# The Hyena short convolution kept in the order of the tokens, with TensorE's transposes taking every eighth column of it

## The chip, the cores and the metric

The kernel runs on one core of a Trainium2 chip. The metric is the device time of one execution in microseconds; the profile is one execution taken by the hardware profiler. Its engines are TensorE (PE, with its weight loads as PEld), VectorE (DVE), ScalarE (ACT), GpSimd (POOL) and SyncE (SP), which issues the DMAs.

## The reference, cut to what matters

One layer of an encoder: a SwiGLU half, a mixer of a Hyena branch and an RWKV-7 branch, another SwiGLU half, on 1024 tokens of 1024 features in float32. The change lies in the first step of the Hyena branch, a convolution of width three along the tokens, for each of 1536 channels, and in the layout in which its result is handed to the long convolution.

```python
def _centred_conv3(u, w, b):
    up = jnp.pad(u, ((0, 0), (1, 1), (0, 0)))
    return w[0] * up[:, :-2] + w[1] * up[:, 1:-1] + w[2] * up[:, 2:] + b
...
    uc = _centred_conv3(u, conv_w, conv_b).astype(jnp.float32)
    x1, x2, v = jnp.split(uc, 3, axis=-1)
```

## The kernel before, in words

The mixer's input projection is computed column tile by column tile. A tile is 128 channels; `column` multiplies it out for two halves of 512 tokens with split float32r operands (`mm3`, lines 43 to 45), 24 matmuls into each PSUM bank `pw`, of which there are three. The first twelve tiles are the Hyena ones, in the order 8 to 11 (v), 0 to 3 (x1) and 4 to 7 (x2). Behind each of them stands `hyena_short_conv`.

In that function the channels lie on the partitions and the tokens along the free dimension. ScalarE copies each half out of PSUM into `u` (tile `sh_u`, line 505, with a zero column at either end), and writes the middle tap with its bias into `uc` (tile `sh_o`, line 506). VectorE adds the two outer taps, one instruction for each over all 1024 tokens (line 509). Then TensorE transposes `uc` in eight blocks of 128 x 128 (line 515; the block is the stationary operand, which a weight load brings in, and the identity is what moves), four to a PSUM bank (`hy_tp`), ScalarE copies each bank out (line 516) and one DMA writes the tile to DRAM (line 517).

The long convolution behind it works on tokens n = 8 m + r, with m on the partitions and r = 0 to 7 along the free dimension (`RT` is 8). So block r of the transposes must hold the tokens r, r + 8, r + 16 and so on. In the kernel before, `uc` has the shape [128, 8, 128] with r outermost. Lines 506 and 509 write it (and line 509 reads it) through the view `ucv`, whose next element in the order of the tokens lies 128 floats (512 bytes) further; each transposed block is contiguous.

Between the column tiles the program computes the Hyena filters in steps (`hyena_filters`): matmuls `ps_h` (line 376) and `ps_k` (line 404) on TensorE, `kt`, `eo`, `cxt` and `kout` on VectorE, `sq` on ScalarE, `acc` on GpSimd, and DMAs of `kout` to DRAM (`d_kf`). GpSimd also makes the low halves of the weights (`w_lo`, line 37) for the first nine of these tiles. A scheduler sets the order of the instructions on each engine when the program is built; on the chip each engine goes through its own list in order. The RWKV column tiles follow (`rwkv_columns`, `rwkv_tile`): they have the same copy out of PSUM and the same two VectorE taps, in the order of the tokens on both sides (lines 1249 and 1258, tiles also named `sh_u` and `sh_o`).

Of the kernel before, what the change touches and what calls it, by code (L numbers as in the profile page):

```python
# [13 lines left out]
F32 = mybir.dt.float32  # L14
F32R = mybir.dt.float32r
AF = mybir.ActivationFunctionType
ALU = mybir.AluOpType
# [3 lines left out]
P = 128  # L21
L = 1024
# [225 lines left out]
RT = 8  # L248
# [247 lines left out]
def hyena_short_conv(nc, pool, xpool, psum, ident, ps, cw, dst):  # L496


    u = pool.tile([P, L + 2], F32, name="sh_u", tag="sh_u")
    nc.vector.memset(u[:, 0:1], 0.0)  # L500
    nc.vector.memset(u[:, L + 1 : L + 2], 0.0)
    uc = pool.tile([P, RT, P], F32, name="sh_o", tag="sh_o")
    ucv = uc.rearrange("p r m -> p m r")
    for t in range(2):
        nc.scalar.copy(u[:, 1 + 512 * t : 513 + 512 * t], ps[t])
        nc.scalar.activation(ucv[:, ts(t, 64), :], ps[t].rearrange("p (m r) -> p m r", r=RT),
                             AF.Identity, bias=cw[:, 3:4], scale=cw[:, 1:2])
    for j in (0, 2):
        nc.vector.scalar_tensor_tensor(ucv, u[:, j : j + L].rearrange("p (m r) -> p m r", r=RT),
                                       cw[:, j : j + 1], ucv, ALU.mult, ALU.add)  # L510
    o = xpool.tile([P, RT, P], F32, name="sh_x", tag="sh_x")
    for h in range(2):
        pt = psum.tile([P, 4, P], F32, name="hy_tp", tag="hy_tp")
        for q in range(4):
            nc.tensor.transpose(pt[:, q], uc[:, 4 * h + q, :], ident)
        nc.scalar.copy(o[:, 4 * h : 4 * h + 4, :], pt)
    nc.sync.dma_start(dst, o)

# [661 lines left out]
def mixer_in(tc, I, ident, wp, hl, scl, h2, h2ctx, dr):  # L1180
# [3 lines left out]
    with ExitStack() as ctx:  # L1184
# [110 lines left out]
        with ExitStack() as c2:  # L1295
            ptp = c2.enter_context(tc.tile_pool(name="hytp", bufs=2, space=PSUM))
            sx = c2.enter_context(tc.tile_pool(name="shx", bufs=2))
            cw = hyena_vectors(nc, one, I)
            hidden = hyena_hidden(tc, I, h2)
            done = 0  # L1300

            for i, t in enumerate((8, 9, 10, 11, 0, 1, 2, 3, 4, 5, 6, 7)):
                if i < 2:
                    next(hidden)
                elif i == 2:
                    for _ in hidden:
                        pass
                    bg = hyena_filters(tc, c2, I, h2, dr["kf"], scl)
                while i > 1 and (done < i * 3 or (t < 8 and t // 2 >= scl.filters)):
                    if next(bg, bg) is bg:  # L1310
                        break
                    done += 1
                ps = column(t * P)
                if t < 8:
                    nc.vector.tensor_scalar(cw[:, t], cw[:, t], scl.tile[:, t : t + 1], None, ALU.mult)
                hyena_short_conv(nc, two, sx, ptp, ident, ps, cw[:, t], dr["X"][t // 4][:, :, ts(t % 4, P)])
            for _ in bg:
                pass
# [426 lines left out]
```

## Time and profile before

| | |
|---|---|
| median of 3 runs | 2900.08 us (2899.32 to 2900.85) |
| the profiled execution | 2905.31 us, its span 2903.5 us |
| PE busy | 2718.3 us, 94% of the span |
| DVE busy | 1232.0 us, 42% |
| ACT busy | 905.1 us, 31% |
| POOL busy | 555.4 us, 19% |
| mean granted TensorE clock | 0.966 |

The span runs from the first instruction to the last; the 1.8 us between it and the execution's time lie around it. A busy share is an average over the whole program: the twelve Hyena tiles take about a tenth of it. A wait is put down to whatever released it last.

### The profile page before, as it was taken

The page shows a single profiled execution, that of the slowest core. Times are in us where ns is not written, and L with a number is a line of the kernel's source. Part 1 is how long each engine was busy: PE and PEld are TensorE (multiplying, and loading weights), DVE is VectorE, ACT ScalarE, POOL GpSimd, SP SyncE. Part 2 cuts the span into 40 slices and gives each one's busy share as a digit, 9 for nine tenths or more (in the row PEclk, how much of TensorE's full clock was granted, in tenths as well). Part 3 has the DMA queues.
Part 4 walks back from the last instruction along what each step waited for, and adds up shares of the span by engine and source line. Part 5 has one row for each costly group of instructions (what it writes and reads, how often), then busy time and mean ns, then how long its engine had stood idle before and what let it go on. Part 6 is the DMA issues. An engine that isn't in the chain of part 4 may idle for free. (4 is left out here: it accounts for less than half of the span.)

```text
span 2903.5 us, 46061 instructions
## 1 busy us (share of the span) xinstructions
PE 2718.3 (94%) x19440; PEld 2198.2 (76%) x19440; DVE 1232.0 (42%) x2141; ACT 905.1 (31%) x1517; POOL 555.4 (19%) x351
## 2 busy tenths in 40 slices
PE   7999999999689899987899999797999999999998
PEld 6888888888566677775787787675778888888887
DVE  4111110111547669898765566756560111101014
ACT  4111111111445443333554555522332111111112
POOL 2323233232414210000000000000033232223322
PEclk9999999999899999998999999898999999999999
DMA  4111111111342245554445334457631111111102
GB/s 123 51 44 51 44 55 47 41 54 41 112 134 69 91 129 179 149 168 127 135 125 160 102 113 148 145 161 234 189 87 54 49 51 44 55 40 53 48 27 91
DMA packets 408990, 277.49 MB, mean 96 GB/s; under 512 B 51107, under 2 KB 369135, under 8 KB 408144
## 3 DMA queue, kind: packets, MB, share of 16 engines
q1 hardware_dynamic: 408784, 274.55, 31.7%
q8 instruction: 153, 2.51, 0.4%
q14 instruction: 53, 0.43, 0.0%
HBM read 203.58 MB, written 70.91 MB: 95 GB/s over the span
## 5 line engine op out<-in xcount | busy, mean ns | idle before, releaser
L43 PE MATMUL pgu<-hThi,w_hi 128*128 128x512 f32 x1408 | 554.1, 394 | 0.8 <-issue 0.8
L45 PE MATMUL pgu<-hThi,w_lo 128*128 128x512 f32 x1408 | 551.4, 392 | 0.0
L44 PE MATMUL pgu<-hTlo,w_hi 128*128 128x512 f32 x1408 | 548.4, 390 | 0.5 <-DVE hTlo L37 0.3
L210 DVE TENSOR_TENSOR silu<-silu,pgu 128x512 f32<-128x512 f32 x88 | 60.5, 688 | 892.2 <-PE pgu L45 882.7
L33 ACT CAST w_hi<-w_st 128x1024 fp32r<-128x1024 f32 (+1 forms) x180 | 175.5, 976 | 496.2 <-PE pgu L44 320.4
L37 POOL TENSOR_TENSOR w_lo<-w_st,w_hi 128x1024 fp32r<-128x1024 f32 x100 | 240.4, 2404 | 413.2 <-ACT w_hi L33 407.5
L45 PEld LDWEIGHTS pgu<-hThi,w_lo 128*128 128x128 f32 x1408 | 264.6, 188 | 60.5
L44 PEld LDWEIGHTS pgu<-hTlo,w_hi 128*128 128x128 f32 x1408 | 264.6, 188 | 59.1 <-DVE hTlo L37 0.7
L43 PEld LDWEIGHTS pgu<-hThi,w_hi 128*128 128x128 f32 x1408 | 264.7, 188 | 55.8 <-issue 1.2
L43 PE MATMUL pdn<-g_hi,wd_hi 128*128 128x512 f32 x704 | 274.9, 391 | 4.6 <-DVE xT L227 4.6
L44 PE MATMUL pdn<-g_lo,wd_hi 128*128 128x512 f32 x704 | 274.4, 390 | 2.0 <-POOL g_lo L37 2.0
L45 PE MATMUL pdn<-g_hi,wd_lo 128*128 128x512 f32 x704 | 274.8, 390 | 1.5 <-POOL wd_lo L37 1.5
L227 DVE SCALAR_TENSOR_TENSOR xT<-pdn,xT 128x512 f32<-128x512 f32 x192 | 132.4, 691 | 315.3 <-PE pdn L45 315.3
L43 PE MATMUL pw<-hThi,w_hi 128*128 128x512 f32 (+1 forms) x448 | 186.4, 416 | 18.5 <-DVE nm_h L123 10.0
L45 PE MATMUL pw<-hThi,w_lo 128*128 128x512 f32 (+1 forms) x448 | 186.8, 418 | 12.1 <-DVE w_lo L1228 12.1
L37 POOL TENSOR_TENSOR wd_lo<-wdst,wd_hi 128x512 fp32r<-128x512 f32 (+1 forms) x112 | 132.9, 1187 | 332.8 <-ACT wd_hi L33 332.8
L37 POOL TENSOR_TENSOR g_lo<-silu,g_hi 128x512 fp32r<-128x512 f32 x88 | 113.9, 1294 | 397.2 <-ACT g_hi L33 397.2
L44 PE MATMUL pw<-hTlo,w_hi 128*128 128x512 f32 (+1 forms) x448 | 184.6, 412 | 0.0
L33 ACT CAST wd_hi<-wdst 128x512 fp32r<-128x512 f32 (+1 forms) x112 | 64.4, 576 | 379.1 <-PE pdn L44 360.7
L37 POOL TENSOR_TENSOR hTlo<-nm_h,hThi 128x512 fp32r<-128x512 f32 x16 | 23.1, 1444 | 802.9 <-ACT hThi L33 802.9
L43 PEld LDWEIGHTS pdn<-g_hi,wd_hi 128*128 128x128 f32 x704 | 132.2, 188 | 33.2 <-ACT wd_hi L33 4.0
L44 PEld LDWEIGHTS pdn<-g_lo,wd_hi 128*128 128x128 f32 x704 | 132.2, 188 | 30.8 <-POOL g_lo L37 2.9
(312 smaller groups left out, 4245.5 us busy)
## 6 DMA issues: line engine op xcount, KB each, us to landing
w_st<-in_ffn_w_gu SPq DMA_DIRECT2D x88, 512.0 KB, 3.9
w_st<-in_w_in SPq DMA_DIRECT2D x59, 512.0 KB, 4.2
wdst<-in_ffn_w_down SPq DMA_DIRECT2D x64, 256.0 KB, 2.8
wdst<-in_ffn_w_down SPq DMA_DIRECT2D x48, 192.0 KB, 2.5
d_kf<-kout SPq DMA_DIRECT2D x32, 256.0 KB, 2.2
hy_k<-d_kf SPq DMA_DIRECT2D x32, 256.0 KB, 3.2
w_st<-in_w_out SPq DMA_DIRECT2D x16, 512.0 KB, 4.4
d_X<-sh_x SPq DMA_DIRECT2D x12, 512.0 KB, 3.5
```

The costliest lines, as they stand in the source:

```text
L33: nc.scalar.copy(hi, src)
L37: eng.tensor_tensor(lo, src, hi.bitcast(F32), ALU.subtract)
L43: te.matmul(out, lhs[0], rhs[0], start=first, stop=False)
L44: te.matmul(out, lhs[0], rhs[1], start=False, stop=False)
L45: te.matmul(out, lhs[1], rhs[0], start=False, stop=last)
L210: nc.vector.tensor_tensor(sl, sl, pu, ALU.mult)
L227: nc.vector.scalar_tensor_tensor(xa, ps, 0.5, xa, ALU.mult, ALU.add)
```

## The change

`uc` becomes a plain [128, 1024] tile in the order of the tokens. Lines 506 and 509 now write and read it contiguously. The reordering moves to the transposes: block r takes the columns r, r + 8, r + 16 and so on, 128 floats that lie 8 floats (32 bytes) apart, as the stationary operand.

```diff
-    uc = pool.tile([P, RT, P], F32, name="sh_o", tag="sh_o")
-    ucv = uc.rearrange("p r m -> p m r")
+    uc = pool.tile([P, L], F32, name="sh_o", tag="sh_o")
     for t in range(2):
         nc.scalar.copy(u[:, 1 + 512 * t : 513 + 512 * t], ps[t])
-        nc.scalar.activation(ucv[:, ts(t, 64), :], ps[t].rearrange("p (m r) -> p m r", r=RT),
-                             AF.Identity, bias=cw[:, 3:4], scale=cw[:, 1:2])
+        nc.scalar.activation(uc[:, ts(t, 512)], ps[t], AF.Identity, bias=cw[:, 3:4], scale=cw[:, 1:2])
     for j in (0, 2):
-        nc.vector.scalar_tensor_tensor(ucv, u[:, j : j + L].rearrange("p (m r) -> p m r", r=RT),
-                                       cw[:, j : j + 1], ucv, ALU.mult, ALU.add)
+        nc.vector.scalar_tensor_tensor(uc, u[:, j : j + L], cw[:, j : j + 1], uc, ALU.mult, ALU.add)
     o = xpool.tile([P, RT, P], F32, name="sh_x", tag="sh_x")
     for h in range(2):
         pt = psum.tile([P, 4, P], F32, name="hy_tp", tag="hy_tp")
         for q in range(4):
-            nc.tensor.transpose(pt[:, q], uc[:, 4 * h + q, :], ident)
+            nc.tensor.transpose(pt[:, q], uc[:, 4 * h + q :: RT], ident)
         nc.scalar.copy(o[:, 4 * h : 4 * h + 4, :], pt)
```

The numbers of the lines below fall by three; the same instructions stand in the same places of every engine's list. This is VectorE's list around the third tile, before (-) and after (+); `hhx` is a tile of the filters' small network.

```order
 L284 SCALAR_TENSOR_TENSOR hhx<-hhx 64x512
 L285 TENSOR_SCALAR hhx<-hhx 64x512
-L509 SCALAR_TENSOR_TENSOR sh_o<-sh_u,hy_cw,sh_o 128x128x8
+L507 SCALAR_TENSOR_TENSOR sh_o<-sh_u,hy_cw,sh_o 128x1024
 L281 TENSOR_SCALAR hhx<-hhx 64x512
-L509 SCALAR_TENSOR_TENSOR sh_o<-sh_u,hy_cw,sh_o 128x128x8
+L507 SCALAR_TENSOR_TENSOR sh_o<-sh_u,hy_cw,sh_o 128x1024
 L282 TENSOR_SCALAR hhx<-hhx 64x512
```

Nothing moved: the two taps stand where they stood, and only the shape in which they go over the tile is another.

## Rows read from the trace of the kernel before

**Rows 1.** The page: its first line, and the busy time of each engine with its share of the span and its instructions.

```profile
span 2903.5 us, 46061 instructions
...
PE 2718.3 (94%) x19440; PEld 2198.2 (76%) x19440; DVE 1232.0 (42%) x2141; ACT 905.1 (31%) x1517; POOL 555.4 (19%) x351
```

**Rows 2.** The view by stretches of the span: the stage with the short convolution (796 to 1073.5 us), and the one after it. Columns: busy us (and instructions) of PE, PEld, DVE, ACT and POOL, then the granted TensorE clock, the DMA share and GB/s.

```profile
796.00:1073.50 277.50, 252.38 (x1024) 188.52 (x1023) 178.67 (x321) 133.50 (x192) 68.83 (x38) 0.95 0.33 98
1073.50:1375.00 301.50, 264.34 (x1184) 211.68 (x1184) 259.75 (x390) 98.89 (x142) 0.95 (x1) 0.93 0.55 162
```

**Rows 3.** Groups of instructions by line between 795 and 1075 us, different shapes apart. Columns: count, busy us, mean ns of one, idle time of the engine before them and what ended it.

```profile
L509 DVE SCALAR_TENSOR_TENSOR sh_o<-sh_u,hy_cw,sh_o 128x1024 f32<-128x1024 f32 x24 | 50.8, 2116 | 19.9 <-ACT sh_o L506 14.7 <-DMA hf_vec<-in_hy_ffn_b 5.3
...
L506 ACT ACTIVATE sh_o<-pw,hy_cw 128x512 f32<-128x512 f32 x24 | 29.5, 1264 | 4.7 <-DVE hy_cw L1315 4.1 <-DMA hy_cw<-in_hy_conv_b 0.7
...
L515 PE MATMUL hy_tp<-ident,sh_o 128*128 128x128 f32 x96 | 14.8, 305 | 14.9 <-DVE sh_o L509 12.2 <-DVE sh_u L501 2.6
...
L515 PEld LDWEIGHTS hy_tp<-ident,sh_o 128*128 128x128 f32 x96 | 12.0, 155 | 20.0 <-issue 13.0 <-ACT sh_o L506 4.8 <-ACT sh_o L1249 1.9
...
L280 ACT ACTIVATE hhx<-ps_h,hf_vec 64x512 f32<-64x512 f32 x4 | 3.0, 752 | 4.4 <-PE ps_h L331 4.4
```

**Rows 4.** The instructions that write or read a tile named sh_o (minimum, median and maximum ns): two lines of the RWKV part, which use tiles of the same name and size in the order of the tokens.

```profile
L1249 ACT ACTIVATE sh_o<-pw,rw_mu x32: 672/693/702, 1069.9 to 1339.6; 128x512 f32<-128x512 f32 x30, 32x512 f32<-32x512 f32 x2
L1258 DVE SCALAR_TENSOR_TENSOR sh_o<-sh_u,rw_mu,sh_o x32: 1267/1276/1285, 1079.5 to 1352.7; 128x1024 f32<-128x1024 f32 x30, 32x1024 f32<-32x1024 f32 x2
```

**Rows 5.** The view of waits between 795 and 1075 us: who waited for whom, us in total, times, longest.

```profile
PE hy_tp L515 <- DVE sh_o L509: 12.2, 8, 2.5
...
PE pw L43 <- ACT sh_o L506: 2.6, 1, 2.6
```

**Rows 6.** The timeline of TensorE, every matmul group of the stage that this part of the prediction speaks of, each with its wait. Columns: start us, us, engine, line, operation, operands, count, and in brackets the idle time before and its releaser.

```profile
816.87 0.68 PE L43 MATMUL pw<-hThi,w_hi 128*128 128x512 f32 x1 [2.56 <-ACT sh_o L506]
...
835.12 1.06 PE L515 MATMUL hy_tp<-ident,sh_o 128*128 128x128 f32 x8 [1.50 <-DVE sh_o L509]
...
849.40 1.06 PE L515 MATMUL hy_tp<-ident,sh_o 128*128 128x128 f32 x8 [1.50 <-DVE sh_o L509]
...
864.45 1.61 PE L515 MATMUL hy_tp<-ident,sh_o 128*128 128x128 f32 x8 [2.61 <-DVE sh_u L501]
...
897.98 2.02 PE L404 MATMUL ps_k<-eo,hf_F 128*128 128x256 f32 x6 [1.64 <-DVE eo L394]
...
919.36 2.04 PE L376 MATMUL ps_h<-w3b,h 65*128 65x512 f32 x2 [2.40 <-DVE kt L380]
...
956.72 1.72 PE L515 MATMUL hy_tp<-ident,sh_o 128*128 128x128 f32 x8 [1.86 <-DVE sh_o L509]
...
972.10 1.07 PE L515 MATMUL hy_tp<-ident,sh_o 128*128 128x128 f32 x8 [2.46 <-DVE sh_o L509]
...
1008.35 1.94 PE L515 MATMUL hy_tp<-ident,sh_o 128*128 128x128 f32 x8 [2.14 <-DVE sh_o L509]
...
1022.06 1.12 PE L376 MATMUL ps_h<-w3b,h 65*128 65x512 f32 x2 [0.63 <-DVE kt L380]
...
1024.08 1.07 PE L515 MATMUL hy_tp<-ident,sh_o 128*128 128x128 f32 x8 [0.43 <-DVE sh_o L509]
...
1059.81 1.06 PE L515 MATMUL hy_tp<-ident,sh_o 128*128 128x128 f32 x8 [0.84 <-DVE sh_o L509]
...
1071.36 1.06 PE L515 MATMUL hy_tp<-ident,sh_o 128*128 128x128 f32 x8 [1.51 <-DVE sh_o L509]
```

**Rows 7.** TensorE in four stretches right behind such waits, and in one stretch between two of them. Columns: the stretch, its length, PE busy, the granted clock, DMA share, GB/s.

```profile
816.90:820.40 3.50, 3.50 (x9) 0.52 0.71 190
864.80:868.20 3.40, 3.40 (x12) 0.50 0.00 0
957.00:960.40 3.40, 3.40 (x14) 0.50 0.02 5
1008.20:1011.60 3.40, 3.25 (x12) 0.50 0.22 81
961.00:968.00 7.00, 7.00 (x29) 1.00 0.57 198
```

**Rows 8.** The timeline of VectorE and of ScalarE ahead of the transposes that start at 956.72 us.

```profile
951.43 2.08 DVE L509 SCALAR_TENSOR_TENSOR sh_o<-sh_u,hy_cw,sh_o 128x1024 f32<-128x1024 f32 x1 [0.54 <-ACT sh_o L506]
953.41 1.28 DVE L419 SCALAR_TENSOR_TENSOR cxt<-cxt 128x512 f32<-128x512 f32 x2
954.61 1.96 DVE L509 SCALAR_TENSOR_TENSOR sh_o<-sh_u,hy_cw,sh_o 128x1024 f32<-128x1024 f32 x1
...
948.53 1.26 ACT L506 ACTIVATE sh_o<-pw,hy_cw 128x512 f32<-128x512 f32 x1
949.58 0.64 ACT L505 COPY sh_u<-pw 128x512 f32<-128x512 f32 x1
950.12 1.28 ACT L506 ACTIVATE sh_o<-pw,hy_cw 128x512 f32<-128x512 f32 x1
```

**Rows 9.** Instructions elsewhere in the kernel with an operand that is read or written in steps: a 32 x 32 block transpose on VectorE whose source is read in steps of 32 floats (L966), the same operation with both operands in order (L984), and a ScalarE copy that writes every eighth float (L723).

```profile
L966 DVE STREAM_TRANSPOSE rw_lt<-rw_a x8: 1074/1077/1171, 1404.3 to 1887.4; 128x512 f32<-128x512 f32 x8
...
L984 DVE STREAM_TRANSPOSE rw_xt<-rw_t x8: 670/711/714, 1417.6 to 1905.1; 128x512 f32<-128x512 f32 x8
...
L723 ACT COPY hy_zT<-hy_t x16: 617/669/778, 1229.6 to 1368.7; 128x256 f32<-128x256 f32 x16
```

## The prediction

> **What bounds the kernel now.** The page comes first: TensorE is busy for 94% of the span, no other engine for half of it [rows 1]. So a change counts by what it takes from, or adds to, TensorE's own list. The view by stretches then gives the stage in which all of the change lies: 277.5 us, of which PE is busy for 252.4, DVE for 178.7 and ACT for 133.5 [rows 2]. PE is the bound here too, with some 25 us of idle time. The view of waits says who owns a good part of that: the transposes of line 515 waited 12.2 us in eight places for the VectorE taps of line 509, and the projection waited 2.6 us once for a PSUM bank that line 506 had still to read [rows 5]. The timeline of PE places them one by one [rows 6]: nine groups of eight transposes have a wait of 0.43 to 2.61 us in front (one of them is put down to a small fill of `sh_u` that stands right behind the second tap; what is late there is the tap). Of the other waits, the one at 1022.06 us is for `kt`, which stands behind a tap in VectorE's list; those at 897.98 and 919.36 us are for filter steps with no tap in front of them.
>
> The reader should see one more thing there. A group of eight transposes takes 1.06 or 1.07 us in six of the nine places and 1.61, 1.72 and 1.94 us in three. [...]
>
> **The change, part by part.** Nothing is added, and no instruction or DMA changes its place in any list. Three kinds get another access pattern.
>
> The taps on VectorE: 24 of them at a mean of 2116 ns [rows 3]. The same operation on the same size in the order of the tokens is in the trace, line 1258, at 1276 ns [rows 4]. So 0.84 us each, 1.68 a tile.
>
> The middle tap on ScalarE: 24 at 1264 ns [rows 3]. Nearest are line 1249 with a scale alone, 693 ns [rows 4], and line 280 with scale and bias, 752 ns [rows 3]. I take the middle, a saving of 0.54 us each.
>
> Together VectorE loses 20 us and ScalarE 13 us of work, but neither is the bound; it counts where PE waits. The two engines ahead of the group at 956.72 us show the chain [rows 8]: the second middle tap (950.12, 1.28 us), at its end the first outer tap (951.43), 1.28 us of filter work, the second outer tap (954.61 to 956.57), and PE 0.15 us later. One ScalarE and two VectorE instructions of the change lie in it, so it gets 0.54 + 1.68 = 2.2 us shorter. A wait can give back no more than it has. So, from [rows 6] in their order: 835.12 and 849.40 give 1.50 each, 864.45 2.2 of its 2.61, 956.72 all 1.86, 972.10 2.2 of 2.46, 1008.35 all 2.14, 1024.08 0.43, 1059.81 0.84, 1071.36 1.51. The wait for `kt` has one shorter tap in front and gives its 0.63. The wait at 816.87 is for the first of three middle taps and gets one saving, 0.54. The sum is 15.3 us. The waits at 897.98 and 919.36 stay. What is late next at 864.45 and 972.10 is still the tap, by 0.3 to 0.4 us; elsewhere PE is not held by this chain any more.
>
> The clock: three of the closed waits are those behind which it fell. Each 3.4 us at 0.50 does work that takes 1.7 us at 1.00; three times that is 5.1 us. I count it in full, since what is left in front of these groups is at most 0.4 us and groups behind waits of 1.50 us kept the clock. The fall at 816.90 I leave, because 2.0 us of its wait remain.
>
> The transposes: 96 weight loads, in 12 groups, now read 128 floats that lie 32 bytes apart. They stand on PE's own list, one behind the other, so whatever they get longer by is paid in full. No row of the trace shows a weight load with such a step. From below it is nothing. The nearest read in steps is VectorE's block transpose: 1077 ns with its source in steps of 32 floats against 711 with both sides in order, 512 elements, so 0.71 ns an element [rows 9]; over 128 columns 91 ns, and 96 times that is 8.8 us. The dearest row is ScalarE's write in steps, (1264 - 693)/512 = 1.12 ns an element [rows 3, 4]: 143 ns a load, 13.7 us. That a step of only 32 bytes is dear too is seen in line 723, where 256 elements written so take 669 ns [rows 9], more than half of what line 506 needs for 512. I take 8.8, the price of a read.
>
> [...]
>
> The sum: -15.3 - 5.1 + 8.8 = **-11.6 us**. The profiled execution took 2905.3 us (2903.5 of span and 1.8 around it), so 2893.7 like that; it lies 5.2 us above the median of the timed runs, 2900.1. Against that median the forecast is **2888.5 us**, 0.4% faster. What follows the stage is held by PE for most of its time (264 of 301.5 us [rows 2]), and so should start earlier by as much.
>
> **The rivals.**
> *The step costs a weight load nothing.* [...] Against it: every stepped operand that the trace does show is slow. The time would be 2900.1 - 20.4 = 2879.7 us. [...] Chance 0.24.
> *The step costs as much as ScalarE's write, or a bit more.* 143 ns a load gives -20.4 + 13.7 = -6.7 us, 2893.4 us; at 180 ns the gain is 3 us. Chance 0.24, about half of it inside 0.2% of the time before.
> *The waits don't close.* PE, freed at the transposes, could arrive early at the next wait for the filters, whose DVE work and `kout` DMAs are paced by other things. If half of the 15.3 us comes back and no fall of the clock goes away, the sum is -7.7 + 8.8 = +1.1 us, 2901 us. Against it: DVE is busy for 178.7 of 277.5 us and gets 20 us less to do. Chance 0.10.
> *Slower: the longer transposes bring the clock down.* A group of eight would take 1.06 + 0.73 = 1.8 us, in which PE mostly loads. If that made the clock fall behind groups that keep it now, each costs 1.7 us. With no gain from the clock the rest is -6.5 us, so it decides from the fourth new fall on; with the three old falls still there and eight new ones the time is 2900.1 - 6.5 + 13.6 = 2907 us. For it: falls in this stage come behind poor stretches of PE. Against it: a wait of 1.50 us and 1.06 us of transposes together did not bring it down at 835.12 and 849.40. Chance 0.08. (A load that is slower by 214 ns would also eat up the 20.4 us, but no row comes near that.)
>
> **How the numbers follow.** The forecast itself, a step priced between 50 and 120 ns and waits that close, has 0.34; its own range is 2884 to 2892. The range for 8 in 10 goes from the rival without a price (2879.7, less 2 us for further closed waits or a fourth regained fall) to the one whose waits don't close: 2877 to 2901. Within 0.2%, 5.8 us, a measurement of this kernel can hardly tell a time from no change. Faster by more: the forecast, the free step and half of the dear one, 0.34 + 0.24 + 0.12, less a little for mixed cases: 0.68. Within: 0.22. Slower: 0.10.
>
> **What would show it.** In the profile after, the taps take about 1.28 us and the middle taps 0.69 to 0.75; the waits of the transposes for the taps come to under 2 us in all, and no fall of the clock stands behind 864, 957 and 1008 us. The decisive row is the weight load of the transposes: a group of eight takes 1.06 us if the step is free, 1.8 if it costs 91 ns, 2.2 at 143. The prediction is wrong if that group takes over 2.7 us, if waits of the same size appear in front of other matmuls, or if the clock falls behind groups without a wait.

## The result, and the profile after

The changed kernel takes 2882.8 us, median of six runs (2878.5 to 2890.5), the kernel before beside it 2900.5 (2895.5 to 2902.6). The ratio, formed over the single runs, is 0.9945, with a 95% interval of 0.9929 to 0.9960: 16 us, or 0.55%, faster (11.6 to 20.6 us); the two medians differ by 17.7 us. A second measurement on another chip gave 0.9951 (0.9939 to 0.9964). The forecast was 11.6 us faster; direction and range hold, but two terms of the sum were wrong, in opposite directions.

The page after, its first line and the busy times, to be read beside [rows 1]:

```profile
span 2880.0 us, 46061 instructions
...
PE 2710.7 (94%) x19440; PEld 2194.5 (76%) x19440; DVE 1215.7 (42%) x2141; ACT 893.7 (31%) x1517; POOL 551.8 (19%) x351
```

VectorE lost 16 us and ScalarE 11 us of work, and neither is the bound. The stretches show where it counts. This is the stage of the short convolution, whose last transposes now start at 1055.1 us instead of 1072.1, and the one behind it, with the columns of [rows 2]:

```profile
796.00:1056.00 260.00, 245.73 (x1022) 184.66 (x1021) 162.52 (x317) 122.54 (x191) 65.52 (x38) 0.97 0.35 103
1056.00:1360.00 304.00, 265.00 (x1190) 212.33 (x1190) 260.40 (x393) 98.69 (x143) 0.95 (x1) 0.93 0.55 162
```

PE was idle for 25.1 us of the stage before and is for 14.3 now (260.0 - 245.73), and the mean granted clock went from 0.95 to 0.97. The groups that answer to [rows 3], between 795 and 1060 us:

```profile
L507 DVE SCALAR_TENSOR_TENSOR sh_o<-sh_u,hy_cw,sh_o 128x1024 f32<-128x1024 f32 x24 | 32.6, 1360 | 16.8 <-ACT sh_o L505 16.8
L505 ACT ACTIVATE sh_o<-pw,hy_cw 128x512 f32<-128x512 f32 x24 | 18.3, 780 | 5.5 <-DVE hy_cw L1312 4.1 <-DMA hy_cw<-in_hy_conv_b 1.4
...
L512 PE MATMUL hy_tp<-ident,sh_o 128*128 128x128 f32 x96 | 13.5, 286 | 1.4 <-DVE sh_u L501 1.2
...
L512 PEld LDWEIGHTS hy_tp<-ident,sh_o 128*128 128x128 f32 x96 | 12.6, 194 | 5.2 <-issue 4.6
```

A tap takes 1.36 us on average instead of 2.12, a middle tap 0.78 instead of 1.26, and the transposes waited 1.2 us in all instead of 14.8. The mean weight load reads 39 ns longer (194 instead of 155; the mean before is raised by the groups at half clock, and its median is 141). But the timeline of PE, three groups of eight transposes, shows what that is worth:

```profile
834.26 1.05 PE L512 MATMUL hy_tp<-ident,sh_o 128*128 128x128 f32 x8
...
860.81 1.13 PE L512 MATMUL hy_tp<-ident,sh_o 128*128 128x128 f32 x8 [1.19 <-DVE sh_u L501]
...
1054.20 1.13 PE L512 MATMUL hy_tp<-ident,sh_o 128*128 128x128 f32 x8
```

Ten of the twelve groups take 1.05 or 1.13 us (the other two 1.16 and, where the clock fell, 1.48), where it took 1.06 or 1.07 [rows 6]. At most that is 0.07 us for each of 12 groups, 0.8 us. Inside a group the transposes follow each other every 112 ns or so, against 109 before, which is less than the row of a load, so most of the longer row lies under the transpose ahead of it. It shows once a group at most: in five groups the second transpose follows the first only after 183 or 184 ns, where behind a wait of the kernel before it was some 136.

The view of waits, between 795 and 1075 us, as in [rows 5]; first what belongs to this stage in the kernel before, and then after:

```profile
PE ps_h L376 <- DVE kt L380: 3.0, 2, 2.4
PE hy_tp L515 <- DVE sh_u L501: 2.6, 1, 2.6
...
PE ps_k L404 <- DVE eo L394: 1.6, 1, 1.6
```

```profile
PE ps_h L376 <- DVE kt L380: 5.0, 3, 2.5
PE hy_y L584 <- DMA d_r<-sh_o: 3.1, 1, 3.1
...
PE pw L43 <- ACT sh_o L505: 2.9, 1, 2.9
PE ps_k L404 <- DVE eo L394: 2.0, 2, 1.6
PE hy_tp L512 <- DVE sh_u L501: 1.2, 1, 1.2
```

With the waits of [rows 5], and 3.0 us for `ac` in both, the stage's waits come to 25.0 us before and 14.1 after (without that of `hy_y`). The transposes' own are gone. Those for the filters' `kt` and `eo` are longer, and behind the stage stands a wait that hardly existed: the first matmul of the long convolution (`hy_y`), before and after:

```profile
1087.40 0.89 PE L587 MATMUL hy_y<-hy_zz,F 128*128 128x256 f32 x3 [0.57 <-DMA d_r<-sh_o]
```

```profile
1072.89 0.89 PE L584 MATMUL hy_y<-hy_zz,F 128*128 128x256 f32 x3 [3.12 <-DMA d_r<-sh_o]
```

The stage is 17.0 us shorter at its last transposes and 14.5 us at this matmul. Who ended a wait is inferred by the profile. `d_r`, a store of the RWKV part, is no operand of this matmul; `hy_zz` and `F` are, and their loads stand ahead of that store in SyncE's queue (shown further down).

### The profile page after: what moved, and what is told of

Read it like the earlier page. It is cut to its first block, busy times and chain, and to the rows that moved or that the text cites. A ratio compares the mean times of both kernels' runs of the same rounds, so it can differ in the third digit from the quotient of the medians.

```text
span 2880.0 us, 46061 instructions
## 1 busy us (share of the span) xinstructions
PE 2710.7 (94%) x19440; PEld 2194.5 (76%) x19440; DVE 1215.7 (42%) x2141; ACT 893.7 (31%) x1517; POOL 551.8 (19%) x351
```

## The experiments

Ratios are to the kernel before on the same chip. The first four shared a chip, where the kernel before took 2901.8 us; the next four another, where it took 2901.7.

**The step alone, on the old layout.** In the kernel before, the transposes take every eighth column:

```diff
-            nc.tensor.transpose(pt[:, q], uc[:, 4 * h + q, :], ident)
+            nc.tensor.transpose(pt[:, q], uc.rearrange("p r m -> p (r m)")[:, 4 * h + q :: RT], ident)
```

> The kernel before, with nothing changed but the transposes, which now take every eighth column of the tile in the old order (the tokens come out permuted; every size and every wait is as before). My theory after the result is that the step is nearly free: LDWEIGHTS of a transpose reads longer in its row (about 190 ns instead of 141), but a group of eight keeps its length, 1.06 to 1.16 us, and the time is the kernel before's plus 0 to 1 us. The rival is my own forecast, 91 ns for each load, here not hidden by any shorter chain: groups of about 1.8 us and plus 8.8 us (0.3%). At 143 ns it would be groups of 2.2 us and plus 13.7 us (0.5%).

Measured: 2902.0 us, ratio 1.0002 (0.9989 to 1.0014), so between 3.2 us less and 4.1 us more. The transposes in the view by lines, 795 to 1075 us, and one group of the timeline, to be read beside the group at 835.12 in [rows 6]:

```profile
L515 PE MATMUL hy_tp<-ident,sh_o 128*128 128x128 f32 x96 | 14.4, 296 | 14.9 <-DVE sh_o L509 12.6 <-DVE sh_u L501 2.3
L515 PEld LDWEIGHTS hy_tp<-ident,sh_o 128*128 128x128 f32 x96 | 12.2, 196 | 20.6 <-issue 12.6 <-ACT sh_o L506 4.8 <-ACT sh_o L1249 1.9
...
835.12 1.13 PE L515 MATMUL hy_tp<-ident,sh_o 128*128 128x128 f32 x8 [1.50 <-DVE sh_o L509]
```

The group starts at the same 835.12 us, behind the same wait of 1.50, and takes 1.13 us instead of 1.06. Both prices of the prediction, 8.8 and 13.7 us, lie outside the interval. With nothing else changed, no shorter chain can be hiding them.

**Contiguous blocks on the new layout.** The reverse, in the changed kernel:

```diff
-            nc.tensor.transpose(pt[:, q], uc[:, 4 * h + q :: RT], ident)
+            nc.tensor.transpose(pt[:, q], uc[:, ts(4 * h + q, P)], ident)
```

> The changed kernel, with transposes that take blocks of 128 neighbouring columns (the tokens come out in a wrong order; the taps stay as in the changed kernel). If the step is nearly free, LDWEIGHTS falls back to about 141 ns, a group of eight takes 1.06 us, and the time is the changed kernel's or up to 0.8 us less, a ratio to the kernel before of 0.994. If the step costs 91 ns for each load and something else has paid it back, this kernel is 8.8 us under the changed one, a ratio of 0.991.

Measured: 2889.5 us, ratio 0.9960 (0.9947 to 0.9972).

```profile
L512 PE MATMUL hy_tp<-ident,sh_o 128*128 128x128 f32 x96 | 12.7, 275 | 1.3 <-DVE sh_u L501 1.2
L512 PEld LDWEIGHTS hy_tp<-ident,sh_o 128*128 128x128 f32 x96 | 10.6, 141 | 5.4 <-issue 3.7 <-DVE sh_o L507 0.9 <-ACT ex L378 0.4
```

The load is back at 141 ns, and the kernel is no faster than the changed one (0.9945 and 0.9951). The time expected, that of the changed kernel or up to 0.8 us less, was missed by some 7 us, of which the level of this chip explains 1.3 (the kernel before took 2901.8 us here and 2900.5 there). The ratio expected, 0.994, lies just outside the interval, on the side that makes the step look cheaper still. So the step is not what was paid, here either.

**ScalarE's part undone.** The middle tap writes in steps of 128 floats again, in the changed kernel:

```diff
-        nc.scalar.activation(uc[:, ts(t, 512)], ps[t], AF.Identity, bias=cw[:, 3:4], scale=cw[:, 1:2])
+        nc.scalar.activation(uc.rearrange("p (r m) -> p m r", r=RT)[:, ts(t, 64), :], ps[t].rearrange("p (m r) -> p m r", r=RT),
+                             AF.Identity, bias=cw[:, 3:4], scale=cw[:, 1:2])
```

> The changed kernel with one part undone: ScalarE writes its middle tap in steps of 128 floats again, while VectorE's taps and the transposes stay as changed (the tokens come out in a wrong order). My theory is that the gain comes from the chain ahead of the transposes, and that VectorE holds 1.66 us of its 2.14 us and ScalarE 0.48. Taking 1.66 us from the waits of before leaves about 0.5, 0.2, 0.5 and 0.4 us at the waits of 2.2, 1.86, 2.2 and 2.14 us: 1.6 us more than the changed kernel, and up to 3 us more where the clock falls again; 2883 to 2888 us, a ratio to before of 0.994 to 0.996. The rival, that ScalarE's write is what mattered, gives nearly all of the 17.7 us back: a ratio of 0.998 to 1.

Measured: 2891.0 us, ratio 0.9958 (0.9944 to 0.9972). Groups of lines and waits:

```profile
L508 DVE SCALAR_TENSOR_TENSOR sh_o<-sh_u,hy_cw,sh_o 128x1024 f32<-128x1024 f32 x24 | 31.3, 1304 | 19.0 <-ACT sh_o L505 19.0
L505 ACT ACTIVATE sh_o<-pw,hy_cw 128x512 f32<-128x512 f32 x24 | 29.7, 1272 | 4.7 <-DVE hy_cw L1313 4.1 <-DMA hy_cw<-in_hy_conv_b 0.7
...
PE hy_tp L513 <- DVE sh_o L508: 1.1, 2, 0.7
PE hy_tp L513 <- DVE sh_u L501: 0.9, 1, 0.9
```

Its last transposes start at 1054.1 us, against 1055.1 in the changed kernel. ScalarE's 11 us can go back without costing anything that is measured: the transposes wait 2.0 us, where 1.6 were expected on top of the 1.2. The ratio is in the range expected; the time, 2883 to 2888 us, was missed by 3.

**VectorE's part undone.** The taps go through the stepped view again, in the changed kernel:

```diff
-        nc.vector.scalar_tensor_tensor(uc, u[:, j : j + L], cw[:, j : j + 1], uc, ALU.mult, ALU.add)
+        ucv = uc.rearrange("p (r m) -> p m r", r=RT)
+        nc.vector.scalar_tensor_tensor(ucv, u[:, j : j + L].rearrange("p (m r) -> p m r", r=RT),
+                                       cw[:, j : j + 1], ucv, ALU.mult, ALU.add)
```

> The changed kernel with the other part undone: VectorE's two taps read and write their tile in steps of 128 floats again (2.1 us each), while ScalarE's middle tap and the transposes stay as changed (the tokens come out in a wrong order). By my theory only 0.48 us of the chain is gained: the waits of before come back less 0.48 each, about 9.7 us of 14, with the falls of the clock behind them, up to 5 us; 2892 to 2898 us, a ratio to before of 0.997 to 0.999. The rival, that ScalarE's write is what mattered, keeps nearly all of the gain: 2883 to 2886 us, a ratio of 0.994 to 0.995.

Measured: 2899.7 us, ratio 0.9993 (0.9982 to 1.0004).

```profile
L508 DVE SCALAR_TENSOR_TENSOR sh_o<-sh_u,hy_cw,sh_o 128x1024 f32<-128x1024 f32 x24 | 50.6, 2110 | 15.9 <-ACT sh_o L505 15.9
...
PE hy_tp L514 <- DVE sh_o L508: 9.3, 9, 1.6
PE ps_h L376 <- DVE kt L380: 5.6, 3, 2.5
...
PE hy_tp L514 <- DVE sh_u L501: 2.6, 2, 2.3
```

The transposes wait 11.9 us again, and the last ones start at 1071.3. The two halves of the change don't share the gain evenly: VectorE's taps carry it, and ScalarE's write alone is worth 0.07%, not told from nothing. I had expected 0.1 to 0.3%.

**The changed kernel once more.**

> The changed kernel itself once more, to stand beside the three that follow and to be compared with the kernels with one part undone: a ratio to the kernel before of 0.993 to 0.996. If the step of the transposes costs next to nothing, the kernel with contiguous blocks (0.996) is no faster than this one; if it costs 91 ns for each load, this one comes out about 0.3% slower than that, at 0.999.

Measured: 2888.1 us, ratio 0.9951 (0.9939 to 0.9964). It is level with contiguous blocks (0.9960), not 0.3% slower.

**F loaded once.** The long convolution's table F is the one that the filters use; its second load goes, and an outer pool holds the first.

```diff
...
-            F = hy.tile([P, RT, 2, P], F32, name="F")
-            nc.sync.dma_start(F, I["c_fwd"])
```

> The changed kernel with the 1 MB table F loaded once and held, instead of a second time behind the filters. In the trace of the changed kernel the first matmul of the long convolution waits 3.12 us for a transfer, where before it waited 0.57: my theory is that this wait is given-back gain, since the second load of F and the transfer of hy_zz behind it are held by the filters' last stores, which did not move with the transposes. Without the second load the wait falls under 1 us and the time by 2 to 3 us against the changed kernel, a ratio to before 0.001 lower. The rival is that the first operand itself (d_X, or the filters' d_kf) lands late in any case: the wait stays at about 3 us and the time is the same.

Measured: 2885.9 us, ratio 0.9942 (0.9927 to 0.9957). The wait at the long convolution stays:

```profile
PE hy_y L582 <- DMA hy_zz<-d_X: 2.4, 1, 2.4
```

It is 2.4 us instead of 3.4 and is now put down to `hy_zz`, the other operand. But the edit was no clean test. The scheduler answered it with another order on TensorE (18 matmuls of line 45 instead of 23 in the 22 us around the last transposes), and the last transposes start at 1061.7 us, 7.8 later than in the changed kernel on the same chip (1053.9). The theory missed its number (under 1 us), and the rival, a wait of about 3 us, came closer. The time, 2.2 us under the changed kernel on this chip, is the one that the theory expected, but with another order on TensorE it says nothing of either.

**The low halves of the weights on VectorE.** The rows ahead of the new wait at 957.29 us in the changed kernel, on VectorE and on GpSimd:

```profile
953.69 0.42 DVE L480 TENSOR_TENSOR kout<-cxt 128x256 f32<-128x256 f32 x1
953.72 2.62 POOL L37 TENSOR_TENSOR w_lo<-w_st,w_hi 128x1024 fp32r<-128x1024 f32 x1 [10.47 <-ACT w_hi L33]
...
954.04 2.60 DVE L481 TENSOR_TENSOR kout<-cxt 128x256 f32<-128x256 f32 x1
956.55 0.68 DVE L380 TENSOR_TENSOR kt<-ps_h,ex 128x512 f32<-128x512 f32 x1
...
957.29 0.70 PE L376 MATMUL ps_h<-w3b,h 65*128 65x512 f32 x1 [2.03 <-DVE kt L380]
```

The same subtraction takes 0.42 us and then 2.60, beside GpSimd's split, which ends at 956.34; `kt` comes behind it, and PE behind that. So 2.2 us are lost in this row; what makes it long is not shown by any run. My theory for the experiment: without a split beside them such rows take 0.4 us again, the waits for `kt` and `eo` fall by 3 to 6 us together, and the time by 2 to 6 us. The experiment moves the splits of all twelve Hyena tiles away from GpSimd (three of them come before this stage, nine in it):

```diff
-            w = col_weights(nc, wp, I["w_in"][:, c0 : c0 + width], KD, width)
+            w = col_weights(nc, wp, I["w_in"][:, c0 : c0 + width], KD, width, lo_eng="dve")
```

> The changed kernel with the low halves of the ten Hyena column weights split on VectorE (1.22 us each in a row of the same shape) instead of GpSimd (2.4 us each). In the trace of the changed kernel the remaining waits of TensorE for kt and eo (2.46 us at 912.70, 2.03 at 957.29, 1.63 at 892.83) stand right behind VectorE rows that take 2.3 to 2.6 us instead of 0.4 while GpSimd's split runs. [...]

Measured: 2883.4 us, ratio 0.9935 (0.9916 to 0.9953). The small scaling of `hy_cw` on VectorE in the changed kernel and in this one (minimum, median, maximum ns):

```profile
L1312 DVE TENSOR_SCALAR hy_cw<-hy_cw,scl x8: 210/211/2299, 890.2 to 1036.1; 128x4 f32<-128x4 f32 x8
```

```profile
L1312 DVE TENSOR_SCALAR hy_cw<-hy_cw,scl x8: 210/211/217, 887.6 to 1026.0; 128x4 f32<-128x4 f32 x8
```

The waits for `kt` fall from 4.9 us (in the changed kernel on this chip) to 2.5, those for `eo` from 3.6 to none, and the row of 2.30 us is gone. Both together fall by 6.0 us, where 3 to 6 were expected. The last transposes start at 1046.7 us, 7.2 earlier than in the changed kernel. In the time this is 4.7 us between the medians, as expected, but only 0.16%, and the intervals overlap. The edit also gave the scheduler another order, so the 7.2 us are not all shown to come from these rows.

**Both edits.** Those of the last two experiments together.

```diff
...
-            nc.sync.dma_start(F, I["c_fwd"])
...
-            w = col_weights(nc, wp, I["w_in"][:, c0 : c0 + width], KD, width)
+            w = col_weights(nc, wp, I["w_in"][:, c0 : c0 + width], KD, width, lo_eng="dve")
```

> Both edits together, F loaded once and the split on VectorE. If both theories hold, the gains add to 4 to 9 us against the changed kernel: 2874 to 2879 us where the changed one takes 2883, a ratio to before of 0.991 to 0.993. If neither holds, the changed kernel's ratio.

Measured: 2877.8 us (2869.8 to 2882.9), ratio 0.9914 (0.9899 to 0.9930). That is 10.3 us under the changed kernel on the same chip (2884.0 to 2891.2, no overlap): a version that is faster than the kernel before and the changed one. Time and ratio lie in the ranges expected, but which part is due to what stays open, since the order differs; its long convolution waits 4.4 us for `hy_zz`.

**The price of a step by itself.** Groups of 16 on a resident tile, added to the changed kernel (a shortened piece):

```diff
+                for q in range(16):
+                    te_.transpose(pt[:, q % 4], hf[:, 0 : 8 * P : 8], ident)
...
+                for q in range(16):
+                    te_.matmul(pt[:, q % 4], ident, hf[:, 0 : 8 * P : 8], start=True, stop=True)
```

> The changed kernel with a block added ahead of the third of its last column tiles: nine groups of 16, each on a line of its own, whose results nobody reads. Six groups are transposes of a resident tile whose 128 columns stand 1, 2, 4, 8, 16 and 32 floats apart; three are float32 matmuls of 128 columns against the identity, whose moving columns stand 1, 8 and 32 floats apart. It prices the step by itself. If the step is nearly free, as the kernels with one part undone say, the transposes of a group follow each other every 100 to 115 ns at every step, and only the row of LDWEIGHTS is longer from some step on (141 to about 190 ns). If a step costs once it is longer than the 8 of the changed kernel, the groups of 16 and 32 are longer than the one of 8, by up to 91 or 143 ns for each load. The rival of the forecast (91 ns at 8 floats, hidden elsewhere in the kernel) would show here as 16 transposes in 3.1 us or more, where contiguous ones take 1.7.

Measured in one execution, so without a comparison of times. The stretches of PE, one group each (a neighbour's row or two counted with them): transposes at steps of 1, 2, 8 and 32 floats, then float32 matmuls, each of two passes (96 rows for the 48 of them), with moving columns 1, 8 and 32 floats apart. Columns: the stretch, its length, PE busy and rows, clock, DMA share, GB/s.

```profile
986.88:988.60 1.72, 1.72 (x17) 1.00 0.00 0
988.62:990.53 1.91, 1.91 (x18) 1.00 0.15 31
992.46:994.24 1.78, 1.78 (x18) 1.00 0.05 9
996.08:997.88 1.80, 1.80 (x18) 1.00 0.15 58
997.89:1001.45 3.56, 3.56 (x34) 1.00 0.56 213
1001.46:1008.90 7.44, 7.44 (x34) 1.00 0.28 107
1008.91:1015.95 7.04, 7.04 (x33) 1.00 0.01 2
```

From the starts of the single rows, the transposes follow each other every 109, 120, 120, 113, 113 and 113 ns at steps of 1, 2, 4, 8, 16 and 32 floats: up to 11 ns for a step, and not more for a long one (115 ns at most had been expected; steps of 2 and 4 take 120). A pass with a stepped moving operand takes 233 or 220 ns instead of 112. So a price of the size that I had put on the weight load, 91 to 143 ns, does show on TensorE, but at the other operand: 121 and 108 ns a pass.

## Why the prediction was right, and where it was wrong

What bounds the stage was read rightly: PE's waits for VectorE's taps [rows 5, 6]. Undoing VectorE's part alone takes the gain away, undoing ScalarE's does not. By the terms of the sum, in us, for two pairs of executions: the two profiled ones, and the kernel with the step alone against the changed kernel once more, which differ in the outer and middle taps only:

| term | predicted | before to after | step alone to changed |
|---|---|---|---|
| waits in the stage | -15.3 | -10.9 (25.0 to 14.1) | -14.0 (27.7 to 13.7) |
| the clock (half the time at half clock) | -5.1 | -5.7 | -3.7 |
| the step | +8.8 | +0.8 at most | both have it |
| first matmul of the long convolution | 0 | +2.5 | +3.1 |
| sum | -11.6 | -13.3 | -14.6 |
| start of that matmul, as seen | | -14.5 | -14.5 |

The clock is counted up to that matmul: 17.2 to 9.8 us at half clock in the second pair. The ratios of that pair, 1.0002 and 0.9951, are 14.8 us apart, which agrees with its sum.

**The step** is the mis-sized term: 8.8 us predicted, 0.8 at most in the timeline, and no more than 4.1 by the interval of the kernel that has nothing else. The step of the argument that failed is the choice of the nearest row. I priced a weight load by a stepped read of VectorE and a stepped write of ScalarE [rows 9], because every stepped operand that the trace showed was slow. None of them was a stationary operand. The decisive row was named rightly: a group of eight takes 1.05 to 1.13 us, the value that the prediction gave for the rival of the free step. That rival had 0.24, my estimate, and was right on the step; its time, 2879.7 us, was not reached because of the terms below. Nor is a load's longer row paid in full: it went from 141 to about 195 ns, and inside a group the transposes follow each other every 112 ns or so, against 109.

**The waits.** In front of the transposes the forecast was 14.2 us, and 13.6 were given back (14.8 to 1.2); under 2 us were to be left. The 0.54 us at 816.87 did not come: that wait is 2.89 us now. ScalarE's first middle tap there starts when a load of `hy_cw` has landed, at 815.61 us before and at 815.60 after, while PE stood ready 0.8 us earlier. In the changed kernel once more the tap had not to wait for that load, and PE waited 1.4 us. And the waits for `kt` and `eo` went from 4.6 to 7.0 us, where I had let 0.63 go (0.52 of that one is left). The sign that I had named for a wrong prediction, waits of the same size in front of other matmuls, so came true in part. It is no plain give-back, though: the kernel with the step alone, whose order and taps are those of before, has 5.5 us for `kt` too. There the subtraction of line 481 takes 598 ns on average, where in the kernel before it takes 508.

**The clock.** The three falls that I had named [rows 7] went, but others came. The groups that answer to those at 864.45, 956.72 and 1008.35 start at 860.81, 946.88 and 996.02 us after. Stretches after, behind these three and, third in order, behind the wait for `kt` at 957.29:

```profile
861.00:864.40 3.40, 3.40 (x18) 2.49 (x17) 2.01 (x4) 3.25 (x6) 0.00 (x0) 1.00 0.00 0
946.90:950.30 3.40, 3.40 (x20) 2.99 (x20) 2.25 (x6) 1.77 (x4) 0.00 (x0) 1.00 0.10 29
959.00:962.40 3.40, 3.40 (x12) 2.72 (x11) 3.24 (x8) 0.98 (x2) 0.00 (x0) 0.51 0.83 270
996.10:999.50 3.40, 3.40 (x19) 2.96 (x20) 2.20 (x6) 1.72 (x3) 0.00 (x0) 1.00 0.28 107
```

The three groups keep the clock, but a fall comes at 959, behind a wait for `kt` that the profile before does not have there. Taken in short stretches from 796 to 1075 us, the time at half clock is 27.7, 17.2 and 23.3 us in the three profiles with long taps (before, the step alone, VectorE's part undone) and 16.3, 12.6, 12.6 and 10.2 in the four with short ones (the changed kernel twice, ScalarE's part undone, contiguous blocks). The means differ by 9.8 us, 4.9 of time, close to the predicted 5.1; but the first two, whose lists differ only in the step of the transposes, are 10.5 us apart, so a fall read in a single profile is no sure gain, and that the size of the term came out is not shown to be more than chance. Only the fall behind 864 us is in all three with long taps (a granted clock of 0.50, 0.54 and 0.54) and in none of these four with short ones (1.00 in the changed kernel and with contiguous blocks).

**Behind the stage** I had said that what follows should start earlier by as much. The first matmul of the long convolution gave 2.5 to 3.1 us back. The queue of SyncE shows the load that it needs, before and then after:

```profile
1073.73 1.75 SPq L482 DMA_DIRECT2D d_kf<-kout  x2
1078.53 0.33 SPq L1343 DMA_DIRECT2D F<-in_c_fwd  x1
1078.92 0.58 SPq L699 DMA_DIRECT2D hy_zz<-d_X  x1
```

```profile
1057.10 2.27 SPq L482 DMA_DIRECT2D d_kf<-kout  x2
1063.59 0.33 SPq L1340 DMA_DIRECT2D F<-in_c_fwd  x1
1063.98 0.58 SPq L696 DMA_DIRECT2D hy_zz<-d_X  x1
```

From the last transposes (1072.1 and 1055.1) to the load of F it is 6.4 us before and 8.5 after, and `hy_zz` lies right behind. So 2.1 of the 2.5 us go with the later issue of these loads behind the last stores. What holds them, the landing of `d_X` or of the filters' `d_kf`, wasn't settled.

Taken together, the forecast of -11.6 us came close to the -13.3 of the terms because 8.0 us too much for the step stood against 6.9 us too little for waits that stay or appear. That the two errors nearly cancel is luck. In the profiled executions the rest of the program is another 9 us shorter at its end (23.5 us of span in all). The timed medians, 17.7 and 13.7 us, do not confirm that part; the profiled execution of the kernel before was itself 5.2 us above its median.

## What to carry to other kernels

Where a reordering is needed, the stationary operand of a transpose is a place to try for the step: here it cost up to 11 ns a load at steps up to 32 floats, while the same reordering cost VectorE 0.76 us on average for each of 24 taps (2.12 to 1.36). Price a stepped access by a row of the same operand of the same engine; where there is none, keep both ends, and don't let a slow row of another engine pick the value. And sum up what a closed wait uncovers: the next wait of the same engine, and the first transfer behind the stage.

## What the runs showed of the hardware that I had not expected

- A weight load's row and its place on the path are two things: the row went from 141 to about 195 ns, and a group of eight transposes at full clock got longer by 0.07 us at most (1.06 to 1.13).
- A stepped moving operand took a float32 pass of 128 columns from 112 to 233 ns at 8 floats and to 220 at 32, a stepped stationary operand a transpose from 109 to 113 at both. A step of 2 or 4 floats (120 ns) was no cheaper than one of 32.
- A VectorE subtraction of 128 x 256 took 2.60 us instead of 0.42 while GpSimd subtracted 128 x 1024 beside it, and a scaling of 128 x 4 2.30 instead of 0.21. With these splits on VectorE the first was 1.49 at most and the second 0.22.
- The time at half clock in this stage was 27.7 us in one execution and 17.2 in another, of two kernels with the same lists that differ only in the step of the transposes.
